# Stores to DRAM scratch issued from GpSimd's queue, and GpSimd's own work moved to ScalarE and VectorE

## The chip, the cores and the metric

The kernel runs on one core of one Trainium2 chip. The metric is the device time of one execution in microseconds (us). Three runs of the kernel before gave 2695.03 us in the median, from 2694.9 to 2701.88. The profile is one more execution of the same program.

The names of the engines in the profile: PE is TensorE's matmuls and PEld its weight loads, DVE is VectorE, ACT is ScalarE, POOL is GpSimd, SP is SyncE. SPq and POOLq are the queues of instructions of SP and POOL from which DMAs are issued. An engine works through its own instructions in order; before each it waits for the semaphores that the instruction names.

## The reference, cut to what matters

One layer of a streaming encoder for 2048 frames (SEQ) of width 1024, in float32:

```
h = rmsnorm(x, norm_mix_w)
u_b, u_c, u_h, z, xbc, dt_raw = split(h @ w_in)           # 5648 columns
y_a = u_b * conv3(u_c * u_h)                              # short gated convolution
xs, B, C = split(silu(conv4(xbc)))                        # causal, along the frames
dt = softplus(dt_raw + dt_bias)
y_b = ssd_scan(xs, dt, -exp(a_log), B, C) + d_skip * xs   # in chunks, a running state
y_b = grouped_rmsnorm(y_b * silu(z), norm_w)
x = x + concat(y_a, y_b) @ w_out                          # 2048 -> 1024
hid = square(relu(rmsnorm(x, norm_mlp_w) @ w_up))         # 1024 -> 4096
x = x + hid @ w_down                                      # 4096 -> 1024
return rmsnorm(x, final_norm_w)
```

## The kernel before

**Matrix products.** Operands are split in a high and a low part of the type fp32r, `hi` by a cast on ScalarE and `lo` by a subtraction on VectorE, and one float32 product is three matmuls: hi·hi, hi·lo, lo·hi (`mm3`, lines L113 to L115, or L270 to L272). The large products are cut in two by two blocks and calculated with seven products in place of eight (`Seven.chain`); the sums of blocks that this needs are made on VectorE, for weights in `combine`, for activations in `prepare` and `sums`. Weights come from DRAM through `load_w` (a DMA into one of three `wraw` buffers, L95) and `split_w` (L100 on ScalarE, L101 on VectorE).

**Stages.** In the profile, times from the start of the span: 0 to 485 us the norm and the first half of the input projection; 485 to 985 its second half, with chunks 0 to 15 of the scan beside it; 985 to 1310 the output projection, with chunks 16 to 31 of the scan beside it; 1310 to 1440 the rest of the output projection and the entry into the MLP (its normed input is made, its first weights are loaded); 1440 to 2050 the first product of the MLP; 2050 to 2694 the second one and the final norm.

**DRAM scratch.** SBUF doesn't hold the activations, so most results of a stage are stored to DRAM and loaded by the next stage: the sums of the normed input (`hm_d`, `hn_d`, L373/L374), sums of weights (`sums_d`, L234/L240), outputs of the projection (`sz_d`, `ys_d`, `xs_d`, L506 and L651 to L726), the small arrays of the scan (`rd_d`, `dt_d`, L636/L638), the scan's result (`yn_d`, L1274), the residual stream (`x1_d`, named x_d in the profile, L1428), the hidden activations (`hid_d`, L825/L826, and `b12_d`, L822) and the unnormed end result of the first half (`fin_d`, L955). All these DMAs, loads and stores alike, are issued by SP. A store waits at the head of SP's queue until the engine that makes its data is done, and what stands behind it waits too.

**The convolutions.** `Proj.pair` copies the last two or three columns of the half before (`halo`, `halo_s`) in front of a tile, and `conv` and `short` copy the last columns of the new tile back: 80 copies of 128x3 or 128x2 elements on GpSimd (L643, L654, L672, L675).

**The scan.** `Scan.back` takes one of 32 chunks: matmuls `yo`, `st`, `yd` on TensorE; four instructions on VectorE (L1252 to L1255); two on GpSimd (L1258 adds the skip term, L1259 multiplies with the gate); the square on ScalarE (L1262), two sums on VectorE, the sum over partitions as a matmul into `pss` (L1268), the root and reciprocal, and the last product (L1273), which is stored (L1274).

**The output projection.** `Output.unit` runs 64 times, 24 matmuls each. A unit issues the load of the residual tile of the unit after it (L1407, three `xt` buffers; units 32 to 63 load what units 0 to 31 have stored), adds the product to its own (L1427) and stores it (L1428). Units 48 to 63 issue beside it `prepare` for the MLP, and units 62 and 63 its first weights (`load_w`, L95).

**What sets the order.** The kernel is written with the Tile framework. The Python code only issues the work; a scheduler of the framework puts each engine's instructions in an order of its own, by when it thinks that their operands are there, and sets the semaphores. So a change of an instruction's engine can move other instructions as well. DMAs of SP use eight semaphores in turn (DMAHW0 to DMAHW7 in the order below); DMAs of GpSimd have eight of their own (DMASW0 to DMASW7).

## Time and profile before

| | us |
|---|---|
| median of three runs | 2695.03 |
| span of the profiled execution | 2694.2 |
| TensorE busy with matmuls in it | 2610.2 |
| VectorE busy | 1979.4 |
| ScalarE busy | 1381.7 |
| GpSimd busy | 141.5 |
| 16 DMA engines, mean share of the span | 58% |

The profiled execution is as long as the runs' median, within 0.9 us. Rows of the windows view give one stretch of the span: start and end, its length, then busy time and number of instructions of PE, PEld, DVE, ACT and POOL, the granted clock of TensorE (1.00 is full speed), the mean busy share of the DMA engines and GB/s. Rows of the waits view say which engine and line stood idle for what, how long in total, how often, and the longest. In rows of the timeline the number in brackets is the engine's idle time ahead of the instruction, and what ended it; a "xN" at the end of a name means N such instructions in a row, with their time together. An issue of a DMA on SPq takes the time that stands in its row; the data arrive later.

### The profile page before, as it was taken

How to read it: one execution, taken by the hardware profiler on the slowest of the kernel's cores; microseconds unless marked ns; L12 is line 12 of the kernel's file. 1: busy time of each engine (PE TensorE's matmuls, PEld its weight loads, DVE VectorE, ACT ScalarE, POOL GpSimd, SP SyncE). 2: the span in 40 equal slices, each digit the busy share in tenths (PEclk: the TensorE clock that was granted, in tenths of full speed). 3: DMA queues.
4: the chain of work that ended last, by engine and by line, in shares of the span. 5: the costliest groups of instructions: out<-in, count | busy, mean ns of one | idle time of the engine just before them, and what ended most of it. 6: DMA issues, size and time to landing. Idle time of an engine off the chain costs nothing.

```text
span 2694.2 us, 33500 instructions
## 1 busy us (share of the span) xinstructions
PE 2610.2 (97%) x12024; PEld 2125.7 (79%) x12024; DVE 1979.4 (73%) x2687; ACT 1381.7 (51%) x2042; POOL 141.5 (5%) x162
## 2 busy tenths in 40 slices
PE   7999999999999999998999999999999999999998
PEld 5778888678887878776877788788887888888777
DVE  7997677667768766666658856765657887888985
ACT  6633345666567566757326445654545333334433
POOL 0000000011111001111000000000000000000001
PEclk9999999999999999999999999999999999999999
DMA  3575335555555588867596844644348544665752
GB/s 143 189 287 193 141 141 186 183 167 167 171 165 168 161 265 264 250 204 215 191 328 235 312 168 149 228 167 167 143 162 277 160 148 153 205 213 172 238 199 75
DMA packets 288262, 522.27 MB, mean 194 GB/s; under 512 B 25696, under 2 KB 141408, under 8 KB 288096
## 3 DMA queue, kind: packets, MB, share of 16 engines
q1 hardware_dynamic: 288096, 520.14, 57.8%
q8 instruction: 94, 1.54, 0.2%
q14 instruction: 72, 0.59, 0.1%
HBM read 349.65 MB, written 170.39 MB: 193 GB/s over the span
## 4 chain that ended last, share of the span: by engine, by line
PE 57%; issue 25%; DMA 7%; DVE 5%; ACT 3%; POOL 1%; SPq 1%; POOLq 0%; DVEq 0%; ACTq 0%
PE px L270 8%; PE px L272 8%; PE px L271 8%; PE py L270 4%; PE py L271 4%; PE py L272 4%; PE pm L113 3%; PE pm L114 3%; PE pm L115 3%; PE pw L270 2%; PE pw L272 2%; PE pw L271 2%; DMA dec<-rd_d 1%; DVE wlo L101 1%; PE yd L1243 1%
## 5 line engine op out<-in xcount | busy, mean ns | idle before, releaser
L270 PE MATMUL px<-uh,whi 128*128 128x512 f32 x1672 | 660.2, 395 | 27.3 <-DVE xt L1427 7.9
L272 PE MATMUL px<-uh,wlo 128*128 128x512 f32 x1672 | 654.1, 392 | 9.0 <-DVE wlo L101 9.0
L271 PE MATMUL px<-ul,whi 128*128 128x512 f32 x1672 | 653.9, 391 | 0.0
L270 PEld LDWEIGHTS px<-uh,whi 128*128 128x128 f32 x1672 | 315.7, 189 | 106.8 <-issue 16.4
L101 DVE TENSOR_TENSOR wlo<-wraw,whi 128x1024 fp32r<-128x1024 f32 x230 | 233.6, 1016 | 198.5 <-ACT whi L100 195.0
L272 PEld LDWEIGHTS px<-uh,wlo 128*128 128x128 f32 x1672 | 315.5, 189 | 78.3 <-DVE wlo L101 11.9
L271 PEld LDWEIGHTS px<-ul,whi 128*128 128x128 f32 x1672 | 315.9, 189 | 63.9
L100 ACT CAST whi<-wraw 128x1024 fp32r<-128x1024 f32 x230 | 203.1, 884 | 303.4 <-PE px L271 194.6
L100 ACT CAST whi<-s 128x1024 fp32r<-128x1024 f32 x210 | 219.2, 1044 | 226.8 <-PE py L271 89.9
L270 PE MATMUL py<-uh,whi 128*128 128x512 f32 x836 | 327.2, 391 | 2.2 <-ACT whi L100 2.2
L272 PE MATMUL py<-uh,wlo 128*128 128x512 f32 x836 | 325.7, 390 | 0.6 <-DVE wlo L101 0.5
L271 PE MATMUL py<-ul,whi 128*128 128x512 f32 x836 | 325.9, 390 | 0.0
L101 DVE TENSOR_TENSOR wlo<-s,whi 128x1024 fp32r<-128x1024 f32 x210 | 255.9, 1219 | 39.5 <-ACT whi L100 38.8
L113 PE MATMUL pm<-uh,whi 128*128 128x512 f32 (+1 forms) x648 | 252.9, 391 | 2.1 <-ACT uh L204 2.1
L114 PE MATMUL pm<-ul,whi 128*128 128x512 f32 (+1 forms) x648 | 249.1, 384 | 0.0
L115 PE MATMUL pm<-uh,wlo 128*128 128x512 f32 (+1 forms) x648 | 248.8, 384 | 0.0
L315 ACT CAST uh<-rh 128x1024 fp32r<-128x1024 f32 (+1 forms) x128 | 120.3, 944 | 144.2 <-PE py L272 123.0
L270 PEld LDWEIGHTS py<-uh,whi 128*128 128x128 f32 x836 | 156.9, 188 | 36.4 <-ACT whi L100 3.8
L272 PEld LDWEIGHTS py<-uh,wlo 128*128 128x128 f32 x836 | 156.9, 188 | 34.8 <-DVE wlo L101 1.9
L271 PEld LDWEIGHTS py<-ul,whi 128*128 128x128 f32 x836 | 157.0, 188 | 32.5 <-issue 0.2
L270 PE MATMUL pw<-uh,whi 128*128 128x512 f32 x418 | 163.6, 391 | 0.0
L272 PE MATMUL pw<-uh,wlo 128*128 128x512 f32 x418 | 163.2, 390 | 0.0
(215 smaller groups left out, 3798.8 us busy)
## 6 DMA issues: line engine op xcount, KB each, us to landing
hid_d<-e SPq DMA_DIRECT2D x96, 512.0 KB, 3.3
rh<-hid_d SPq DMA_DIRECT2D x96, 512.0 KB, 4.2
wraw<-w_in SPq DMA_DIRECT2D x68, 512.0 KB, 3.8
wraw<-w_up SPq DMA_DIRECT2D x64, 512.0 KB, 5.0
wraw<-w_down SPq DMA_DIRECT2D x104, 256.0 KB, 3.6
dec<-rd_d SPq DMA_DIRECT2D x32, 512.0 KB, 5.4
wraw<-w_out SPq DMA_DIRECT2D x32, 512.0 KB, 5.2
x_d<-xt SPq DMA_DIRECT2D x64, 256.0 KB, 3.7
```

Of the source, the lines that this page charges most:

```text
L100: nc.scalar.copy(hi, raw)
L101: eng.tensor_tensor(out=lo, in0=raw, in1=hi.bitcast(F32), op=ALU.subtract)
L113: nc.tensor.matmul(out, whi, hi, start=(k == 0), stop=False)
L114: nc.tensor.matmul(out, whi, lo, start=False, stop=False)
L115: nc.tensor.matmul(out, wlo, hi, start=False, stop=(k == nk - 1))
L270: nc.tensor.matmul(p, hi, h[0], start=bool(first and k == 0), stop=False, **kw)
L271: nc.tensor.matmul(p, hi, h[1], start=False, stop=False, **kw)
L272: nc.tensor.matmul(p, lo, h[0], start=False, stop=(k == len(g) - 1), **kw)
L315: nc.scalar.copy(p[i][0], t)
L1243: nc.tensor.matmul(yd[(i % 2) * 64 : (i % 2) * 64 + 64, (i // 2) * L : (i // 2 + 1) * L], byhead(t["xdt"])[:, i, :], t["dec"][:, i, :], st ...
```

## The change

- 419 DMAs that store to DRAM are issued by GpSimd (`nc.gpsimd.dma_start`) and no longer by SP: every store but the last ones of the kernel (L1070, in `norm_out`).
- The 80 halo copies of the convolutions run on ScalarE in place of GpSimd.
- The scan's two instructions on GpSimd (L1258, L1259; 32 times each) run on VectorE.

What GpSimd keeps of its own instructions are the constants at the start and the products of `norm_out` (L1065). Arithmetic, tiles, buffers and all loads are the same. Cut to one place of each kind:

```
@@ -231,13 +231,13 @@
             if kept is not None:
-                nc.sync.dma_start(kept[:, 0], s12)
+                nc.gpsimd.dma_start(kept[:, 0], s12)
...
@@ -370,8 +370,8 @@
                 for i in range(3):
-                    nc.sync.dma_start(self.stored[h][k][:, 2 * i : 2 * i + 2], ts[i])
-                nc.sync.dma_start(self.stored[h][k][:, 6], t4)
+                    nc.gpsimd.dma_start(self.stored[h][k][:, 2 * i : 2 * i + 2], ts[i])
+                nc.gpsimd.dma_start(self.stored[h][k][:, 6], t4)
...
         def conv(self, h, q, buf):
 
-            nc.gpsimd.tensor_copy(self.halo[:, q, 0:3], buf[:, TH : TH + 3])
+            nc.scalar.copy(self.halo[:, q, 0:3], buf[:, TH : TH + 3])
...
             for i, e in enumerate((e0, e1, e2)):
-                nc.sync.dma_start(hid_d[h][q][:, 2 * i : 2 * i + 2], e)
-            nc.sync.dma_start(hid_d[h][q][:, 6], t4)
+                nc.gpsimd.dma_start(hid_d[h][q][:, 2 * i : 2 * i + 2], e)
+            nc.gpsimd.dma_start(hid_d[h][q][:, 6], t4)
...
             t3 = t1.rearrange("p (j l) -> p j l", j=4)
-            nc.gpsimd.tensor_tensor(out=t3, in0=t3, in1=t["xd"], op=ALU.add)
-            nc.gpsimd.tensor_tensor(out=y, in0=t3, in1=y, op=ALU.mult)
+            nc.vector.tensor_tensor(out=t3, in0=t3, in1=t["xd"], op=ALU.add)
+            nc.vector.tensor_tensor(out=y, in0=t3, in1=y, op=ALU.mult)
...
             nc.vector.tensor_tensor(out=t, in0=pm, in1=t, op=ALU.add)
-            nc.sync.dma_start(x1_d[b][:, d], t)
+            nc.gpsimd.dma_start(x1_d[b][:, d], t)
```

The same edit stands at L506, L636, L638, L651, L713 to L726 (stores of the projection), L822, L955, L1110 (the first half of the output) and L1274.

What the edit does to the order is seen at two places. In the rows, each name carries the number of its tile, the shape follows, and the brackets hold the semaphores that are waited for.

The first place is SP's queue at the entry into the MLP, where units 61 to 63 of the output projection end and the first weights of the MLP (`wraw_11851`, `wraw_11853`) are loaded. Before:

```order
L1428 DMA x1_d3_80<-xt_11689 128x512 [waits DMAHW1_49]
L1407 DMA xt_11777<-x1_d3_80 128x512 [waits DMAHW2_49]
L1428 DMA x1_d2_79<-xt_11740 128x512 [waits DMAHW3_49,DVE_49]
L95 DMA wraw_11851<-w_up 128x1024
L1407 DMA xt_11822<-x1_d2_79 128x512 [waits DMAHW4_49,DMAHW0_49]
L1428 DMA x1_d3_80<-xt_11777 128x512 [waits DMAHW5_49,DMAHW1_49,DVE_49]
L95 DMA wraw_11853<-w_up 128x1024 [waits DMAHW6_49]
```

In the changed kernel the rows around the same two loads on SP's queue are these:

```order
L1407 DMA xt_11437<-x1_d3_80 128x512 [waits DMAHW1_49,DMASW2_49,DVE_49]
L360 DMA nb_11429<-x1_d0_77 128x512 [waits DMAHW2_49,DMASW3_49,DVE_49]
L95 DMA wraw_11851<-w_up 128x1024 [waits DMAHW3_49,DVE_49]
L360 DMA nb_11432<-x1_d1_78 128x512 [waits DMAHW4_49,DMASW4_49]
L360 DMA nb_11431<-x1_d1_78 128x512 [waits DMAHW5_49,DMASW5_49]
L360 DMA nb_11430<-x1_d0_77 128x512 [waits DMAHW6_49,DMASW6_49]
L1407 DMA xt_11484<-x1_d2_79 128x512 [waits DMAHW7_49,DMASW7_49]
L1407 DMA xt_11521<-x1_d3_80 128x512 [waits DMAHW0_49,DMASW0_49,DVE_49]
L360 DMA nb_11499<-x1_d0_77 128x512 [waits DMAHW1_49,DMASW1_49,DVE_49]
L95 DMA wraw_11853<-w_up 128x1024 [waits DMAHW2_49,DVE_49]
```

The stores of `xt` are gone from this queue, and the two loads of weights stand among the loads for units whose `xt` carry numbers about 11437 to 11521, where before they stood among those of `xt_11777` and `xt_11822`: counted in loads alone, they moved ahead by 21 to 27.

The second place is VectorE's queue in one chunk of the scan during the output projection. `state1` and `stmp` are the scan's, `ul0` and `xt` belong to the output projection. Before:

```order
L1254 TENSOR_TENSOR state1_3802<-state1_3802,st_10418 128x512 [waits DVE_49,PE_49]
L1255 TENSOR_TENSOR stmp_10429<-stmp_10429,yd_10420 128x512 [waits PE_49]
L1373 TENSOR_TENSOR ul0_10613<-ry_10476,uh0_10612 128x512 [waits DMAHW3_49,Activation_49]
L1271 RECIPROCAL srstd_10436<-srstd_10436 128x128 [waits Activation_49]
L1373 TENSOR_TENSOR ul0_10618<-ry_10476,uh0_10617 128x512
L1273 TENSOR_TENSOR y_10145<-y_10145,srstd_10436 128x512 [waits DMAHW1_49,DVE_49]
L1263 TENSOR_TENSOR stmp_10530<-stmp_10530 128x256 [waits Activation_49]
```

After:

```order
L1254 TENSOR_TENSOR state1_3802<-state1_3802,st_10418 128x512 [waits DVE_49,PE_49]
L1255 TENSOR_TENSOR stmp_10429<-stmp_10429,yd_10420 128x512 [waits PE_49]
L1373 TENSOR_TENSOR ul0_10613<-ry_10476,uh0_10612 128x512 [waits DMAHW0_49,Activation_49]
L1271 RECIPROCAL srstd_10436<-srstd_10436 128x128 [waits Activation_49]
L1258 TENSOR_TENSOR stmp_10429<-stmp_10429,xd_10085 128x512 [waits DMAHW1_49,DVE_49]
L1273 TENSOR_TENSOR y_10145<-y_10145,srstd_10436 128x512 [waits DVE_49]
L1259 TENSOR_TENSOR y_10341<-stmp_10429,y_10341 128x512 [waits DMAHW3_49,DMASW2_49,DVE_49]
L1373 TENSOR_TENSOR ul0_10618<-ry_10476,uh0_10617 128x512
L1427 TENSOR_TENSOR xt_10381<-pm_10447,xt_10381 128x512 [waits DMAHW2_49,DMASW1_49,PE_49]
L1263 TENSOR_TENSOR stmp_10530<-stmp_10530 128x256 [waits Activation_49]
```

The two instructions L1258 and L1259 stand between the scan's other instructions, and the sum L1263, which needs the square of L1259's result, comes behind one addition of the output projection (L1427) that stood later before.

## What the time will be, predicted before the change was run

> **What bounds the kernel now.** I read the totals first, then busy time by stage, then what TensorE waited for, then what SP's queue waited for. The totals and the six stages:
>
> ```profile
> PE 2610.2 (97%) x12024; PEld 2125.7 (79%) x12024; DVE 1979.4 (73%) x2687; ACT 1381.7 (51%) x2042; POOL 141.5 (5%) x162
> core 0: 2694.2 us, clock 0.992
> 0.00:485.00 485.00, 457.58 (x1990) 371.81 (x1991) 380.06 (x520) 233.69 (x303) 25.72 (x49) 0.99 0.51 185
> 485.00:985.00 500.00, 495.53 (x2457) 397.82 (x2456) 361.46 (x496) 322.67 (x542) 59.45 (x72) 1.00 0.55 172
> 985.00:1310.00 325.00, 310.24 (x1623) 248.97 (x1622) 206.32 (x310) 203.53 (x403) 47.73 (x32) 0.99 0.78 233
> 1310.00:1440.00 130.00, 120.50 (x520) 98.64 (x519) 87.78 (x109) 43.12 (x55) 0.00 (x0) 0.96 0.79 275
> 1440.00:2050.00 610.00, 604.58 (x2649) 496.99 (x2649) 416.63 (x542) 329.91 (x446) 0.00 (x0) 1.00 0.54 194
> 2050.00:2694.00 644.00, 621.78 (x2793) 511.46 (x2791) 527.17 (x714) 248.82 (x296) 8.59 (x9) 0.99 0.56 181
> ```
>
> TensorE bounds the kernel: it is busy for 2610.2 of 2694.2 us. No matmul is added or taken away, so at most the 84.0 us between the two can be won, of which some 27 us lie in the first stage (485 less 457.58) and 22 us in the last (644 less 621.78). VectorE, at 73%, comes second. These are the waits of TensorE that could hang on SP's queue or on VectorE's; the second group is the part from 20 to 485 us alone, the third 1310 to 1440, the last 2050 to 2680:
>
> ```profile
> PE px L272 <- DVE wlo L101: 9.0, 6, 3.1
> PE px L270 <- DVE xt L1427: 7.9, 1, 7.9
> PE pss L1268 <- DVE facc L1441: 7.0, 1, 7.0
> ...
> PE px L272 <- DVE wlo L101: 5.1, 3, 3.1
> PE px L270 <- ACT whi L100: 2.6, 1, 2.6
> ...
> PE px L270 <- DVE e L838: 1.5, 1, 1.5
> ...
> PE px L270 <- DVE acc L969: 6.4, 9, 1.3
> PE px L272 <- DVE wlo L101: 2.6, 1, 2.6
> PE px L270 <- ACT whi L100: 2.1, 1, 2.1
> ```
>
> They are small and spread out, with two of 7 to 8 us. The larger is the entry into the MLP, where the first product needs a buffer that the last addition L1427 sets free. What SP and VectorE did there:
>
> ```profile
> 1398.35 0.40 SPq L1428 DMA_DIRECT2D x_d<-xt  x1
> 1398.79 0.45 SPq L95 DMA_DIRECT2D wraw<-w_up  x1
> 1400.65 0.32 SPq L1407 DMA_DIRECT2D xt<-x_d  x1
> 1403.24 0.32 SPq L1428 DMA_DIRECT2D x_d<-xt  x1
> 1403.61 0.43 SPq L95 DMA_DIRECT2D wraw<-w_up  x1
> ...
> 1408.48 0.69 DVE L231 TENSOR_TENSOR s<-wraw 128x512 f32<-128x512 f32 x1 [1.24 <-DMA wraw<-w_up]
> ...
> 1411.57 2.36 DVE L101 TENSOR_TENSOR wlo<-s,whi 128x1024 fp32r<-128x1024 f32 x2 [0.46 <-ACT whi L100]
> 1413.85 4.63 DVE L316 TENSOR_TENSOR ul<-rb,uh 128x1024 fp32r<-128x1024 f32 x4
> 1418.39 0.69 DVE L1427 TENSOR_TENSOR xt<-pm,xt 128x512 f32<-128x512 f32 x1
> ```
>
> Each load of `w_up` was issued right behind a store `x_d<-xt`, which had stood at the head of the queue until its addition was done. VectorE then idled 1.24 us for the second load (issued 1403.61, used 1408.48), and had to do the weight sums, `wlo` and four `ul` in one piece before the last addition at 1418.39. TensorE resumed at 1419.22 with the granted clock down:
>
> ```profile
> 1413.00:1423.00 10.00, 3.78 (x9) 3.04 (x10) 8.97 (x9) 5.88 (x7) 0.00 (x0) 0.52 0.84 282
> ```
>
> The four running microseconds of this row went at 0.52, which costs about 2 us on top of the 7.9 us.
>
> **The change part by part.** First the stores. Waits of SP's queue that are for data to be stored, and then what one store costs and how long it takes to land:
>
> ```profile
> SPq L825 <- DVE e L208: 258.4, 85, 11.1
> SPq L1428 <- DVE xt L1427: 51.7, 38, 3.2
> SPq L1407 <- DMA x_d<-xt: 51.6, 31, 3.8
> ...
> x_d<-xt SPq DMA_DIRECT2D x64, 256.0 KB, 3.7
> xt<-x_d SPq DMA_DIRECT2D x32, 256.0 KB, 4.3
> ```
>
> SP loses 419 issues of 0.32 to 0.40 us (the rows of L1428), some 134 to 168 us of queue time, and the waits above (258.4 and 51.7 us of them) go to GpSimd's queue, where no load stands behind them. SP's own time is worth nothing by itself, since nothing but DMAs runs there; it counts only where a load came late. In the first product of the MLP, TensorE is busy 604.58 of 610 us in spite of the 258.4 us, so there they are worth at most 5.4 us; I take nothing. The wait of 51.6 us is a dependence (a load of what a store has just written) and stays.
>
> What is late at the entry into the MLP is the weights. In the new order both loads of `w_up` stand 21 to 27 loads earlier on SP's queue, and VectorE's weight sums stand ahead of the last units' work. In the stage before, 1310 to 1440, VectorE has 130 − 87.78 = 42 us free and can take the sums and `wlo` there. What is left then at the border is the last addition (0.69 us) and the hops around it, about 1.4 us as in the smallest waits above (1.3, 1.5), so 6.5 us of the 7.9 go. The clock, which fell only in long idling, should then not fall: another 2 us. The wait of 1.5 us on L838 right behind it I leave.
>
> In the first stage, VectorE is busy 78% and the 5.1 and 2.6 us of waits for weights lie where `prepare` stores `hm_d` between the loads: loads that no longer queue behind those stores are worth perhaps a fifth of 7.7 us, 1.5 us. The same kind at the start of the last stage, 2.6 and 2.1 us, I put at 0.8 us, and another 0.6 us near 481, where the stage's last loads of `hm_d` come.
>
> What does a store cost on GpSimd? No row of before shows a DMA issued there. The nearest ones are SP's 0.32 us per issue, GpSimd's smallest copy and its large instructions:
>
> ```profile
> L643 POOL COPY halo<-buf 128x3 f32<-128x3 f32 x24 | 9.3, 390 | 271.2 <-DVE buf L692 271.2
> L1258 POOL TENSOR_TENSOR stmp<-stmp,xd 128x512 f32<-128x512 f32 x32 | 46.8, 1462 | 558.6 <-DVE stmp L1255 315.5 <-issue 115.8 <-DMA bc<-xs_d 35.4
> L1259 POOL TENSOR_TENSOR y<-stmp,y 128x512 f32<-128x512 f32 x32 | 44.9, 1403 | 2.5
> L1253 DVE TENSOR_TENSOR state<-state,dd 128x512 f32<-128x512 f32 x32 | 21.9, 684 | 0.2 <-PE yo L1238 0.2
> L1211 ACT COPY btok<-ptb 128x128 f32<-128x128 f32 x32 | 8.5, 267 | 0.0
> ```
>
> I take 0.5 us, a little above the copy, since an issue moves no data through the engine. Ends: 0.32 us and 1.46 us. 419 stores are then 134, 210 or 612 us of a queue that is otherwise nearly empty. A store is late by 0 to 1.1 us (1.46 less 0.32), or, since it no longer waits behind loads on SP, somewhat early. Who feels it is the loop over `x_d` in units 32 to 63 alone: addition 0.69, store 3.7, load 4.3, together 8.7 us. The load is issued one unit ahead, and what it loads was stored by a unit at least three before; a unit is 24 matmuls, at 610/2649 = 0.230 us each 5.5 us, so three are 16.6 us, with 7.9 us to spare. A delay of 1.1 us is hidden: nothing.
>
> By the Trainium skill, page "DMA: Bandwidth & Descriptors", section Specifications, the first byte of a transfer from GpSimd's software descriptors comes at about 1 us against about 0.6 us for the hardware's; no run here shows it yet, and by an estimate from it a store would land 0.4 us later, which leaves the sum as it is.
>
> Halo copies: 80 leave GpSimd (0.39 us each) for ScalarE, at 0.27 us by the copy L1211, together 21 us on an engine that is busy 51%. In the two stages where they lie it is busy 233.69 of 485 and 322.67 of 500. A copy could hold up the cast `whi` behind it by 0.27 us; if one in eight did so at a moment when TensorE waits, that is 10 × 0.27 = 2.7 us; I take 0.7 us, and 0 to 5 us as ends.
>
> The scan: 64 instructions leave GpSimd, where they took 1.46 and 1.40 us, for VectorE at 0.69 us: 64 × 0.684 = 43.8 us, half each in 485 to 985 and 985 to 1310. VectorE goes there from 361 to 383 of 500 us and from 206 to 228 of 325 us, still under 77%. What hides them is this free time; if it is gone where a burst stands, 1.37 us per chunk shows. On the other side the chunk's chain gets shorter by 1.46 + 1.40 − 1.37 = 1.5 us and one change of engine. The chain counts at the other large wait, `pss` behind `facc`:
>
> ```profile
> 1248.29 1.26 POOL L1258 TENSOR_TENSOR stmp<-stmp,xd 128x512 f32<-128x512 f32 x1 [13.85 <-DVE stmp L1255]
> 1246.98 0.55 SPq L1173 DMA_DIRECT2D dec<-rd_d x1
> 1253.38 0.40 ACT L1218 ACTIVATE dec<-dec,dd 128x128 f32<-128x128 f32 x1 [1.82 <-DMA dec<-rd_d]
> 1254.30 0.69 DVE L1441 TENSOR_TENSOR facc<-sq,facc 128x512 f32<-128x512 f32 x1 [1.68 <-ACT sq L1440]
> ```
>
> `dec` was issued late, at 1246.98, and all else waited behind it on ScalarE. With a shorter chain and an SP queue without stores it could come 2 us earlier, and the wait of 7.0 us shrink by that. Against it I set 1.3 us for VectorE's 1.37 us showing in about one chunk of 32. Of the stage I keep −2 for that wait and, with the copies' 0.7, +2 for costs.
>
> The sum: −6.5 − 2 (entry into the MLP) − 1.5 − 0.6 (first stage) − 0.8 (last stage) − 2 (scan) + 2 = −11.4 us. Against the profiled 2694.2 that is 2682.8; the runs' median is 0.8 us above the span, so 2683.6, said as 2683.5 us.
>
> **The rivals.**
>
> *No change.* TensorE's waits are bursts of VectorE, and loads that come earlier only wait in their buffers: with three `wraw` buffers a load can be issued early only when a buffer comes free, and the new order may find it taken. Then the 7.9 us stay but for 1.24 us of idling, and the rest is noise: −1.2 + 2 − 2 gives about 2694, with 2691 to 2699 around it. Against it speaks that the store at 1398.35 stands directly ahead of the load at 1398.79. By the Trainium skill, "DMA: Bandwidth & Descriptors", section "Issuing engines are not separate DMA queues", another issuing engine saves only the sequencer's time for the issue; that is this rival's mechanism, and the 258.4 us of SP that cost TensorE at most 5.4 us agree with it.
>
> *Slower: stores queue up on GpSimd.* Its queue is in order as SP's is. In units 48 to 63 the stores of `hn_d` (four per step of `prepare`) and of `x_d` share it. If a store takes 2 us there in place of 0.5, four of them hold an `x_d` store up for 8 us and lengthen its own issue by 1.7; with 7.9 us to spare, the loop is short by 1.8 us in each of 16 units: 29 us less the gain of 11.4, about 2713. It decides from about 1.65 us per store on (four are 6.6 us, the longer issue 1.3). For it speaks that GpSimd's instructions in the profile take about twice VectorE's time (1462 against 684 ns); against it that an issue moves no tile, and the copy of 390 ns.
>
> *Slower: VectorE too full.* If the 1.37 us per chunk shows in each of 16 chunks of the output projection, where the additions L1427 set free the buffers that TensorE needs, that is 22 us less the gain of 11.4: about 2705. VectorE's 63% in that stage speaks against it.
>
> **How the numbers follow.** My forecast has a chance of 0.52: about half the sum rests on one wait whose release moved plainly in the order. No change has 0.18. Stores that queue up have 0.20, since their price has no row at all, and a full VectorE 0.10. A difference of 0.3%, 8.1 us, is about what a measurement of this kernel can tell from no change, so 2686.9 and 2703.1 divide the cases: faster 0.52, same 0.18, slower 0.30. My forecast's own range is 2668 (the 7.0 us too and half of the first stage's waits gone, −26) to 2687 (the clock not won, copies at 4 us). The range reaches over no change to the full VectorE, with some spread, to 2708; outside are most of the stores that queue up and the forecast's own ends.
>
> **What would show it.** The entry into the MLP right: loads of `w_up` issued on SP well before 1395 us, and the wait of `px` on L1427 under 2 us with the clock near 1.0 in those 10 us. Stores right: issues on POOLq around 0.5 us, landing within 1 us of 3.7, no wait of L1407 longer than now. Copies right: about 0.27 us each on ScalarE, and waits for `whi` no longer. Scan right: L1258 and L1259 at 0.69 us on VectorE, and less than 2 us more of waits of TensorE for VectorE between 485 and 1310. The prediction is wrong if an issue on GpSimd takes over 1.5 us, if TensorE's busy time itself changes, or if VectorE's other instructions get longer while GpSimd issues stores.

## The result, and the profile after

The changed kernel takes 2741.41 us in the median (2737.48 to 2743.27, four runs), beside 2697.03 us for the kernel before on the same chip: a ratio of 1.016, with a 95% interval from 1.0145 to 1.0174. It is slower by 44 us, where the prediction said 11 us faster, and it lies above the range.

The totals of the changed kernel's page, with the row of its core, answer to the first rows of the prediction:

```profile
PE 2626.3 (96%) x12024; PEld 2136.6 (78%) x12024; DVE 2010.2 (73%) x2751; ACT 1390.4 (51%) x2122; POOL 242.8 (9%) x437
core 0: 2740.0 us, clock 0.984
```

TensorE does the same 12024 matmuls. Its busy time grew by 16.1 us, since a matmul takes longer at a lower granted clock, and its idle time by some 30 us. Both have the same places here: in the rows below the clock is 1.00 in 150 us without a wait, and 0.50 and 0.51 in two short pieces that lie right behind waits of 8.4 and 7.2 us; a matmul takes 150 / 664 = 0.23 us at 1.00 and 4.81 / 11 = 0.44 us at 0.50. The windows view of the kernel before, 150 us in the middle of the MLP's first product:

```profile
1570.00:1720.00 150.00, 150.00 (x662) 123.89 (x661) 90.60 (x119) 75.81 (x104) 0.00 (x0) 1.00 0.41 146
```

The same view of the changed kernel, in the middle of that product, at its beginning, and two short pieces of the beginning:

```profile
1600.00:1750.00 150.00, 150.00 (x664) 124.24 (x663) 90.78 (x119) 75.84 (x105) 15.63 (x30) 1.00 0.41 150
1430.00:1565.00 135.00, 114.65 (x466) 92.56 (x467) 97.84 (x131) 63.83 (x85) 19.88 (x37) 0.89 0.70 246
1434.00:1439.00 5.00, 4.81 (x11) 3.80 (x12) 4.05 (x5) 1.72 (x2) 0.54 (x1) 0.50 0.80 229
1547.00:1556.00 9.00, 5.30 (x12) 3.74 (x13) 9.00 (x15) 3.28 (x4) 1.62 (x3) 0.51 0.77 259
```

In these 150 us in the middle of the product nothing is lost: TensorE is busy for 150 of 150 us with the stores on GpSimd, as it was before. The loss stands at the beginning, where the clock is 0.89 in the mean and 0.50 and 0.51 in the two pieces. Where the 44 us arise is read from the start of one and the same instruction of VectorE in two traces. The table gives its time in the kernel before and how much later it starts (us) in the changed kernel and in four of the experiments told below. Each column is one trace: the kernel "stores alone, order held" and the one with stores from ScalarE (told below) do not differ before the MLP, yet at the last unit of the output projection they stand at +7.6 and +12.1, so a difference of less than 5 us between columns says little.

| place (instruction) | before | changed | moved compute alone | stores alone, order held | all of it, order held | all of it, SP's order free |
|---|---|---|---|---|---|---|
| first unit of the output projection (L1427) | 990 | +5.3 | −2.1 | +1.5 | 0.0 | +4.7 |
| last chunk of the scan (L1254) | 1292 | +6.5 | −9.5 | +5.5 | −5.7 | −0.4 |
| last unit of the output projection (L1427) | 1418 | +15.0 | −10.3 | +7.6 | −3.1 | +7.1 |
| MLP up, 25th addition (L838) | 1594 | +30.3 | −11.7 | +11.1 | −0.7 | +11.5 |
| the same, 46th | 1727 | +33.6 | −11.0 | +11.2 | −0.7 | +11.2 |
| the same, 67th | 1864 | +34.9 | −11.7 | +12.8 | +1.4 | +15.1 |
| the same, 91st | 2017 | +34.9 | −11.6 | +12.8 | +1.4 | +15.1 |
| MLP down, 7th addition (L969) | 2073 | +39.5 | −11.2 | +13.3 | +2.1 | +19.1 |
| the end (L1049) | 2648 | +45.3 | −12.0 | +22.0 | +10.4 | +26.2 |

In the changed kernel, 24 us of the 45 arise between the end of the scan and the first quarter of the MLP's first product, where the normed input is made, stored and loaded again (`prepare`). The rest comes in four pieces of some 5 us each: in the input projection, later in the MLP's first product, at the border to its second, and in the last third of that product.

The largest waits of TensorE in the changed kernel, after the one at the start:

```profile
PE px L270 <- DVE e L838: 12.8, 5, 3.6
PE px L270 <- DVE acc L969: 11.3, 8, 3.6
PE px L272 <- DVE wlo L101: 10.3, 3, 7.2
PE px L270 <- DVE xt L1427: 8.4, 1, 8.4
PE pss L1268 <- DVE facc L1441: 7.8, 1, 7.8
PE px L270 <- ACT s L689: 7.3, 5, 3.5
PE pm L113 <- DVE xt L1427: 6.8, 4, 3.1
PE px L270 <- DVE buf L692: 4.2, 1, 4.2
```

The waits view of its VectorE and of SP's queue, those that changed most:

```profile
DVE nb L364 <- DMA nb<-x_d: 29.8, 10, 5.7
...
SPq L95 <- DVE wlo L101: 813.3, 118, 16.1
SPq L1407 <- DMA x_d<-xt: 156.2, 46, 8.3
```

TensorE waits for nothing that is new in kind: mostly evictions and additions of VectorE that set its buffers free (L838, L969, L692, L1427). VectorE's own wait for loads ahead of the normed input's first step grew from 5.7 us in the kernel before to 29.8. SP's wait for free weight buffers grew from 296.4 to 813.3 us and its wait at the reload of the residual stream from 51.6 to 156.2. These two are no measure of the loss: SP no longer stands at stores and so stands at the next load, and with the old order held (below) they are still 734.6 and 119.1 us.

How the one leads to the other is seen at the first such place. The rows are the timeline's around 155 us in the changed kernel, VectorE's and the matmul that waited:

```profile
154.79 0.75 DVE L364 SCALAR_TENSOR_TENSOR nb<-nb,cv,facc 128x512 f32<-128x512 f32 x1 [5.35 <-DMA nb<-x]
155.46 0.68 DVE L692 TENSOR_TENSOR buf<-px,s 128x512 f32<-128x512 f32 x1
...
156.19 0.65 PE L270 MATMUL px<-uh,whi 128*128 128x512 f32 x1 [4.24 <-DVE buf L692]
```

VectorE's queue held L364, which needs a load, ahead of the addition L692, which sets a buffer of TensorE free. VectorE stood 5.35 us for the load (of the input x, which no store feeds), and TensorE stood 4.24 us for the addition. In the timeline of the kernel before, the additions L692 of this product stand ahead of L364:

```profile
150.36 0.69 DVE L692 TENSOR_TENSOR buf<-px,s 128x512 f32<-128x512 f32 x1 [1.96 <-PE px L272]
153.15 0.69 DVE L692 TENSOR_TENSOR buf<-py,s 128x512 f32<-128x512 f32 x1 [2.10 <-PE py L272]
153.75 1.41 DVE L364 SCALAR_TENSOR_TENSOR nb<-nb,cv,facc 128x512 f32<-128x512 f32 x2
```

### The profile page after: what moved, and what is told of

Its sections match the earlier page's. It is cut to its first block, busy times and chain, and to the rows that moved or that the text cites. A ratio compares the mean times of both kernels' runs of the same rounds, so it can differ in the third digit from the quotient of the medians.

```text
span 2740.0 us, 33639 instructions
## 1 busy us (share of the span) xinstructions
PE 2626.3 (96%) x12024; PEld 2136.6 (78%) x12024; DVE 2010.2 (73%) x2751; ACT 1390.4 (51%) x2122; POOL 242.8 (9%) x437
## 4 chain that ended last, share of the span: by engine, by line
PE 41%; issue 40%; DMA 8%; DVE 6%; POOL 2%; ACT 2%; SPq 0%; POOLq 0%; DVEq 0%; ACTq 0%
PE px L270 6%; PE px L271 6%; PE px L272 6%; PE py L270 3%; PE py L272 3%; PE py L271 3%; PE pm L113 3%; PE pm L114 2%; PE pm L115 2%; PE pw L272 1%; PE pw L271 1%; PE pw L270 1%; DVE wlo L101 1%; DVE ul L316 1%; DMA rb<-hn_d 1%
## 5 line engine op out<-in xcount | busy, mean ns | idle before, releaser
L270 PE MATMUL px<-uh,whi 128*128 128x512 f32 x1672 | 666.5, 399 | 51.9 <-DVE e L838 12.8
L272 PE MATMUL px<-uh,wlo 128*128 128x512 f32 x1672 | 659.1, 395 | 10.3 <-DVE wlo L101 10.3
L272 PEld LDWEIGHTS px<-uh,wlo 128*128 128x128 f32 x1672 | 318.9, 191 | 80.1 <-DVE wlo L101 12.1
```

The costliest lines, as they stand in the source:

```text
L270: nc.tensor.matmul(p, hi, h[0], start=bool(first and k == 0), stop=False, **kw)
L272: nc.tensor.matmul(p, lo, h[0], start=False, stop=(k == len(g) - 1), **kw)
```

## The experiments

My theory after the result was that the stores carry the whole loss, in two shares: they land later, and the scheduler, which took them to cost less, made a worse order of it. The rivals were a VectorE that is too full, and a GpSimd queue that is too slow by itself. "Order held" means that a function at the end of the build draws an edge from each instruction of an engine to the next, in the order of another build; the edges set the order of issue and are of the kind that has no semaphore:

```
+def pin(nc, tc):
...
+    at = {i.name: i for i in nc.cur_bb.bb.instructions}
+    for engine, names in json.loads(zlib.decompress(base64.b85decode(ORDER))).items():
+        here = [at[f"I-{n}"] for n in names if f"I-{n}" in at and engine in str(at[f"I-{n}"].engine)]
+        for a, b in zip(here, here[1:]):
+            tc.add_manual_dep(b, a.name, info, reason="order")
```

In the traces of the kernels held like this, the loads on SP and the instructions of the other three engines do stand in the order that they were held to, without exception. The kernel before with only these edges was not run, so that the edges cost nothing by themselves is not shown. The traces speak for it: in the held kernel told last, whose stores of the hidden activations are on SP, the MLP's first product loses nothing from its 25th addition to its end (+6.6 us behind the kernel before at both ends, within 0.3 us).

### Stores alone, compute alone

The first kernel takes only the stores of the change (against the changed kernel):

```
-            nc.scalar.copy(self.halo[:, q, 0:3], buf[:, TH : TH + 3])
+            nc.gpsimd.tensor_copy(self.halo[:, q, 0:3], buf[:, TH : TH + 3])
...
-            nc.vector.tensor_tensor(out=t3, in0=t3, in1=t["xd"], op=ALU.add)
-            nc.vector.tensor_tensor(out=y, in0=t3, in1=y, op=ALU.mult)
+            nc.gpsimd.tensor_tensor(out=t3, in0=t3, in1=t["xd"], op=ALU.add)
+            nc.gpsimd.tensor_tensor(out=y, in0=t3, in1=y, op=ALU.mult)
```

> Only the 419 stores go to GpSimd's queue; the halo copies and the scan's two instructions stay on GpSimd. Theory 'stores' (the whole loss comes from the stores, of 1310 to 1555 us above all): 2735 to 2745 us, as the changed kernel. Theory 'VectorE too full': 2690 to 2702 us, since the compute that moved is back.

Measured: 2748.22 us beside 2698.15 for the kernel before, ratio 1.0183 (1.0153 to 1.0214). This is 3 us above the range of the first theory and far from the second.

The second takes only the other half, the same lines the other way round, with all stores on SP.

> Only the halo copies and the scan's two instructions are moved; all stores stay on SP. Theory 'stores': 2690 to 2700 us, no difference from before. Theory 'VectorE too full': 2725 to 2740 us.

Measured: 2686.29 us, ratio 0.9958 (0.9941 to 0.9975). It is faster than the kernel before, and 4 us below both ranges. The stores carry the loss, and a VectorE too full is out: the moved compute wins 12 us. A third kernel moves the scan's two instructions alone:

```
-            nc.gpsimd.tensor_tensor(out=t3, in0=t3, in1=t["xd"], op=ALU.add)
-            nc.gpsimd.tensor_tensor(out=y, in0=t3, in1=y, op=ALU.mult)
+            nc.vector.tensor_tensor(out=t3, in0=t3, in1=t["xd"], op=ALU.add)
+            nc.vector.tensor_tensor(out=y, in0=t3, in1=y, op=ALU.mult)
```

> Only the scan's two instructions go to VectorE; halo copies stay on GpSimd and all stores on SP. Theory 'the scan's shorter chain wins the 12 us': 2684 to 2690 us. Theory 'the halo copies' part is half of it': 2690 to 2695 us.

Measured: 2690.02 us beside 2698.62, ratio 0.9965 (0.995 to 0.998). Most of the gain is the scan's; whether the halo copies add the rest can't be told, since the two intervals overlap.

Where the gain is from stands in VectorE's waits. In the kernel before:

```profile
DVE stmp L1263 <- ACT stmp L1262: 65.6, 25, 5.8
```

With the compute moved, this wait, and the groups of the moved instructions:

```profile
DVE stmp L1263 <- ACT stmp L1262: 17.9, 12, 3.7
...
L1258 DVE TENSOR_TENSOR stmp<-stmp,xd 128x512 f32<-128x512 f32 x32 | 21.8, 683 | 0.4
L1259 DVE TENSOR_TENSOR y<-stmp,y 128x512 f32<-128x512 f32 x32 | 22.0, 686 | 0.7
L643 ACT COPY halo<-buf 128x3 f32<-128x3 f32 x24 | 4.6, 191 | 36.7 <-DVE buf L692 36.6
```

VectorE took 43.8 us of work and lost 47.7 us of waiting. While GpSimd did the chunk's two steps, VectorE stood at L1263, whose square comes from their result, and everything behind L1263 stood with it. VectorE's waiting is time of TensorE only in part: TensorE's own waits in the output projection with its chunks of the scan (985 to 1310 us, and 10 us earlier in the faster kernel) fell from 14.8 to 9.0 us, and in the table that stretch wins 7.4 of the 12 us. That the shorter wait at L1263 is what shortened them is argued, not shown.

### Which stores: the two that are reloaded at the costly place

The changed kernel with the stores of the residual stream and of the normed input back on SP:

```
-                    nc.gpsimd.dma_start(self.stored[h][k][:, 2 * i : 2 * i + 2], ts[i])
-                nc.gpsimd.dma_start(self.stored[h][k][:, 6], t4)
+                    nc.sync.dma_start(self.stored[h][k][:, 2 * i : 2 * i + 2], ts[i])
+                nc.sync.dma_start(self.stored[h][k][:, 6], t4)
...
-            nc.gpsimd.dma_start(x1_d[b][:, d], t)
+            nc.sync.dma_start(x1_d[b][:, d], t)
```

> The changed kernel, but the stores of the residual stream (L1428) and of the normed input (L373, L374) are back on SP; the other 299 stores are on GpSimd. Both theories of the stores: 2690 to 2705 us, since the only loops from store to load in 1310 to 1555 us run over these. If the hidden activations' stores (5.1 us to landing) hold the additions L838 up: 2712 to 2725 us.

Measured: 2739.38 us, ratio 1.0148 (1.0118 to 1.0178). Both expectations missed: nothing came back. (307 stores stay on GpSimd here, 112 are back; the expectation says 299.) With the order left to the scheduler, every such variant is a new order, so what the two loops cost by themselves can't be read from it, and from here on the order was held.

### Order held

Only the stores on GpSimd, and the loads on SP and all instructions of VectorE, ScalarE and TensorE in the order of the kernel before (the stores-alone kernel with `pin` called at its end):

> Only the stores are on GpSimd, and the loads on SP and the instructions of VectorE, ScalarE and TensorE are held in the very order of the kernel before. Theory 'order' (the scheduler's new order, with weight loads ahead of the loads of the normed input, makes those late): 2685 to 2700 us. Theory 'landing' (stores from GpSimd land later, 4.4 us against 3.7 for the residual and 5.1 against 3.3 for the hidden activations, and what loads them or reuses their buffers waits): 2728 to 2745 us.

Measured: 2723.81 us, ratio 1.0083 (1.0058 to 1.0109). Between the two theories: about half of the loss stays with the old order (25.7 us against 2698.15), so it goes with the stores themselves, and the other half (2748.22 less 2723.81, 24 us) is the order.

The full change, in the order of the compute-alone kernel:

> The changed kernel in full, with loads on SP and the instructions of VectorE, ScalarE and TensorE held in the order of the kernel that moved the compute alone (2686 us). Theory 'landing plus order' (two shares that add up, as 2724 against 2698 us for the landing alone and 2748 against 2724 us for the order): 2705 to 2716 us, that is 2686 plus about 25. Theory 'the shares do not add' (moved compute only helps where the stores stand on SP): 2722 to 2735 us.

Measured: 2708.15 us beside 2698.62, ratio 1.0034 (1.0019 to 1.005). The shares add up: 2686 and some 22, where the other pair gave 25.7. Now the full change with only the instructions of VectorE, ScalarE and TensorE held, and SP's order free (`pin` without the entry for SP):

> The changed kernel in full, with only the instructions of VectorE, ScalarE and TensorE held in the order of the kernel that moved the compute alone; SP's loads stay in an order of the scheduler's own (262 of 1043 places differ from that kernel's). With SP held as well it was 2708 us, with nothing held 2741. Theory 'VectorE's order' (instructions that need a late load stand ahead of those that free TensorE's buffers): 2705 to 2716 us. Theory 'SP's order' (weight loads that wait for a buffer stand ahead of the loads of the normed input): 2730 to 2742 us.

Measured: 2721.37 us beside 2698.25, ratio 1.0088 (1.0059 to 1.0117). It is between the two: of the 33 us from 2708 to 2741, SP's order of loads makes about 13 and the other engines' order about 20. The division is rough: it goes by which order was set free first, and SP's order in this kernel is not quite the changed kernel's (in the traces, by line and tile name, 182 of its 1019 loads stand in another place than in the kernel held in full, and 66 in another than in the changed kernel).

### What makes a store from GpSimd cost anything

With the order held there is no other change than the issuing queue, and the place of a store among GpSimd's own instructions, which the kernel of 2724 us still has in that queue. In the full change these have moved away, and the stores cost 22 us in place of 26, so they are a small part of it at most. First I suspected where a late landing comes from, and issued the hidden activations' stores from ScalarE:

```
-                nc.gpsimd.dma_start(hid_d[h][q][:, 2 * i : 2 * i + 2], e)
-            nc.gpsimd.dma_start(hid_d[h][q][:, 6], t4)
+                nc.scalar.dma_start(hid_d[h][q][:, 2 * i : 2 * i + 2], e)
+            nc.scalar.dma_start(hid_d[h][q][:, 6], t4)
```

> As the kernel with stores on GpSimd in the order of before (2724 us), but the 131 stores of the hidden activations (L822, L825, L826) are issued by ScalarE. What it tells is where the late landing is from. Theory 'software descriptors': L825's stores land in 3.2 to 3.8 us, as from SP (3.3), and the time is 2712 to 2722 us. Theory 'a second queue': loads and stores share the 16 DMA engines in turn once they stand in two queues, so they land in 4.6 to 5.4 us, as from GpSimd (5.1), and the time is 2720 to 2732 us.

Measured: 2758.04 us, ratio 1.0221 (1.0194 to 1.0249). The last number in a row of the list of DMAs is the median time from issue to landing. In the kernel before:

```profile
hid_d<-e SPq DMA_DIRECT2D x96, 512.0 KB, 3.3
```

With the stores on GpSimd and the order held:

```profile
hid_d<-e POOLq DMA_DIRECT2D x96, 512.0 KB, 5.1
```

With these stores on ScalarE, and behind it what TensorE waited for from 1580 to 1760 us in this kernel:

```profile
hid_d<-e ACTq DMA_DIRECT2D x96, 512.0 KB, 5.3
...
PE px L270 <- ACT s L835: 5.9, 8, 1.2
```

The late landing is not GpSimd's alone: from ScalarE it is as late. The time rose by 34 us more and lies outside both ranges; in the middle of the product TensorE now waits for ScalarE's copies L835, which stand in one queue with the stores. From 1420 to 2080 us this wait is 22.4 us in all, where the order-held kernel with all stores on GpSimd has 0.3.

The timeline shows what the stores meet. In the order-held kernel with all stores on GpSimd, SP issues a weight load 0.23 us after the first store of a group:

```profile
1615.04 0.53 POOL L825 DMA_DIRECT2D hid_d<-e  x1 [15.88 <-DVE e L208]
...
1615.27 0.33 SPq L95 DMA_DIRECT2D wraw<-w_up  x1
```

In the kernel before, the load stood behind the stores on SP:

```profile
1603.28 2.29 SPq L825 DMA_DIRECT2D hid_d<-e  x3
1606.00 0.32 SPq L826 DMA_DIRECT2D hid_d<-t  x1
1606.37 1.12 SPq L95 DMA_DIRECT2D wraw<-w_up  x1
```

To take this collision away and leave the stores on GpSimd, SP was made to wait as before: in each store's old place it reads a few numbers of the stored tile.

```
+    def store(dst, src):
+        nc.gpsimd.dma_start(dst, src)
...
+        head = src[0:1, :, 0:8] if len(src.shape) == 3 else src[0:1, 0:8]
...
+        PROBES.append(nc.sync.dma_start(seen, head).ins.name)
```

> As the kernel with the stores on GpSimd and the order of before (2724 us), but at each place where a store stood in SP's queue SP now issues a read of 8 or 16 numbers from the tile that is stored, into a scratch of its own: SP waits for the same data at the same places as before, and the loads behind start no earlier than before, while the 419 stores themselves go out from GpSimd. Theory 'collision' (loads that SP no longer holds back start together with the stores and share the 16 DMA engines, so that the stores land late): the hidden activations' stores land in 2.6 to 3.8 us and the time is 2692 to 2708 us. Theory 'GpSimd's queue' (a store issued from there lands late by itself): they land in 4.6 us or more and the time is 2718 to 2730 us.

Measured: 2723.26 us beside 2699.08, ratio 1.0094 (1.0068 to 1.0121). The two signs disagree. The landing of `hid_d<-e` fell to 3.7 us, as the collision theory had it, and the time did not move. So the collision makes up most of these 96 stores' lateness (5.1 to 3.7, of 3.3). What it is worth to end it stays open: the 32 smaller stores `hid_d<-t` landed later still (6.2 us, against 5.5 with the order held and 3.5 from SP), the 419 reads are transfers themselves whose cost no run shows, and there was little to win, since the order-held kernel lost only 2 us from the 25th addition to the second product (+11.1 to +13.3 in the table). What is left with SP's waits restored is a later start of GpSimd's stores and perhaps a later landing. The start is plain between the end of an addition and the issue of its store. In the kernel before:

```profile
1406.56 0.68 DVE L1427 TENSOR_TENSOR xt<-pm,xt 128x512 f32<-128x512 f32 x1
1407.27 0.32 SPq L1428 DMA_DIRECT2D x_d<-xt  x1
```

In the changed kernel:

```profile
1419.35 0.68 DVE L1427 TENSOR_TENSOR xt<-pm,xt 128x512 f32<-128x512 f32 x1
1420.44 0.54 POOL L1428 DMA_DIRECT2D x_d<-xt  x1 [7.71 <-DVE xt L1427]
```

SP issued 0.03 us after the end (1406.56 + 0.68 = 1407.24), GpSimd 0.41 us after it (1420.03). In the medians over all stores of this line it is 0.03 and 0.41 us too, and the landing behind it 3.7 against 4.3 us in the last experiment: there a store from GpSimd is done about 0.4 + 0.6 = 1.0 us later. The start is the same, within 0.01 us, in the traces of all kernels told here. The landing is less sure: from SP the stores of this line landed in 3.3 to 4.6 us, by kernel, and from GpSimd in 3.8 to 4.8.

Two last kernels, both in the order of before, divide the stores: on SP, or alone on GpSimd, are the 168 whose data or buffers are wanted again in the same stage (L1428, L373, L374, L1274, L955, L1110).

> Stores on GpSimd in the order of before, but the 168 that are loaded again or whose buffers are reused within the same stage are on SP: residual (L1428), normed input (L373, L374), the scan's result (L1274), end results of the first half (L955, L1110). 251 stores stay on GpSimd: hidden activations, outputs of the projection, weight sums, small arrays. Theory 'loops' (a store from GpSimd starts 0.4 us later and lands 0.3 to 1 us later, and only loops from store to load inside a stage feel it): 2695 to 2705 us. Theory 'all stores': 2708 to 2718 us, about 251/419 of the 25 us.

Measured: 2709.3 us beside 2699.55, ratio 1.0037 (1.0024 to 1.0051), with 251 stores on GpSimd.

> The reverse, in the order of before: only the 168 stores of the loops (L1428, L373, L374, L1274, L955, L1110) are on GpSimd. Theory 'loops': 2715 to 2726 us, nearly the whole 25 us. Theory 'all stores': 2704 to 2713 us.

Measured: 2715.27 us, ratio 1.0064 (1.0047 to 1.0082), with 168. The losses, 9.8 and 15.7 us, add up to that of all 419. The 168 make 62% of it, 0.09 us per store against 0.04 for the rest. So neither theory holds: the loops seem to weigh more, though the two intervals touch, and the others count as well.

No stage carries the share of the stores alone. In the table's two columns with the order held, each counted from the kernel whose order it has, about half of it (11 us) has arisen by the 25th addition of the MLP's first product, some 2 us more by the end of that product, and 8 to 9 us in the second, where GpSimd issues only the 24 stores L955 and L1110. But the kernel with the scan alone moved, whose stores are all on SP, loses 6 us in that stretch as well, so this last part can't be laid to the stores with certainty.

### A faster kernel

The compute-alone kernel beats both. One more step was tried on it, the MLP's first weights two units earlier:

```
-            if n == 62:
+            if n == 60:
                 ahead = mlp.weights(mlp.load_cols(w_up, (0, 1)))
                 next(ahead)
-                ws = take(ahead, 2)
-            elif n == 63:
+            elif n == 61:
+                ws = take(ahead, 2)
+            elif n == 62:
                 ws += take(ahead, 1)
```

> The kernel that moved the compute alone (2686 us), with the MLP's first weights loaded two units earlier and split one unit earlier, so that VectorE does the last addition L1427 of the output projection two `ul` and no weight work later than it could. If the wait of TensorE at the entry into the MLP (7.1 us) is VectorE's weight work: it falls to 2 to 4 us, and the time is 2680 to 2684 us. If it is the loads of the normed input: 2685 to 2688 us.

Measured: 2687.49 us beside 2698.62, ratio 0.9964 (0.9946 to 0.9981): no gain over 2686. The wait at the entry fell only from 7.1 to 6.0 us, so VectorE's weight work is a small part of it, and in the two traces the first product had lost the difference again by its 25th addition (−13.3 against −10.3 us at the last unit, −11.1 against −11.7 there). At the entry VectorE then waited for ScalarE's `uh`, which waited 2.7 us for a load of the normed input (`rb`).

## Why the prediction was wrong, point by point

**The sum.** Against the kernel before, in medians (those of the kernel before beside each experiment lie between 2697.0 and 2699.6, so each figure is good to 2 or 3 us): moved compute −12, stores from GpSimd in an unchanged order +22 (order-held full change less compute alone; +26 by the other pair), SP's new order +13, the other engines' new order +20. Together +43, measured +44; they are differences along one row of kernels, so that they add up is no test of them. My sum had −2 + 2 for the compute, 0 for the delay of the stores, and −11 for all that the new order and the freed queue of SP would bring. The lower end of my range, −26, does not follow from the two terms named beside it: with 7.0 in place of 2 and half of 7.7 in place of 1.5, the −11.4 becomes about −19.

**The step that failed first: "a delay of 1.1 us is hidden: nothing".** The price itself was right: I took 0.5 us for an issue and 0 to 1.1 us of delay. An issue took 0.54 us in the median, and the residual landed in 4.4 us in place of 3.7. But I asked only whether the loop over `x_d` closes in time, and gave it 7.9 us to spare. I did not name what stands behind the waiting load on SP. With the order held, where nothing but the queue differs, this term was not 0 but 22 to 26 us. At the entry into the MLP these rows of the changed kernel, which has the new order too, show how a late store reaches TensorE; the store is the one at 1420.44 above:

```profile
1426.28 0.32 SPq L1407 DMA_DIRECT2D xt<-x_d  x1
1426.69 2.48 SPq L308 DMA_DIRECT2D rb<-hn_d  x4
...
1431.14 1.04 ACT L315 CAST uh<-rb 128x1024 fp32r<-128x1024 f32 x1 [4.19 <-DMA rb<-hn_d]
...
1432.22 1.23 DVE L316 TENSOR_TENSOR ul<-rb,uh 128x1024 fp32r<-128x1024 f32 x1 [3.39 <-ACT uh L315]
1433.36 0.68 DVE L1427 TENSOR_TENSOR xt<-pm,xt 128x512 f32<-128x512 f32 x1
...
1434.19 0.76 PE L270 MATMUL px<-uh,whi 128*128 128x512 f32 x1 [8.37 <-DVE xt L1427]
```

The reload L1407 was issued when the store had landed, 5.8 us after the store's issue. Four loads of the normed input stood behind it, `uh` and `ul` waited for these, and the addition that frees TensorE's buffer stood behind `ul`. The delay of one store doesn't have to break its own loop; it has only to reach a queue's head.

Here it broke the loop as well. What the reload waits for is not its data, as I wrote of the 51.6 us, but one of the three `xt` buffers: in the traces it is never issued before the store of the unit three before has landed, and within 0.1 us behind it in 17 of the 32 reloads before and in 29 of 32 in the changed kernel. So the loop runs over three units, as I took it, but not with 16.6 us: from the end of the addition at 1419.35 to the end of TensorE's last matmul of the unit three later (1425.8) it had 5.8 us, and the start of the store, its landing and the reload took 9.4 (0.4, 5.8 and 3.1), so the tile came some 3.6 us late. My 7.9 us to spare was worked out from the mean length of a unit, and VectorE's additions come in bursts (two of them, L1427, start at 1419.35 and 1420.55).

**"−6.5 − 2 (entry into the MLP)".** The mechanism came as forecast as far as the weights: the first three loads of `w_up` were issued at 1355.49, 1369.45 and 1385.68 us, 22 to 43 us earlier than before, and VectorE's weight sums went ahead. The wait still was 8.4 us and the clock fell to 0.50. My step "what is left then at the border is the last addition" failed: what was late next was the normed input. The run with earlier weights says the same for the kernel without the stores' trouble, 6.0 of 7.1 us left. With the order held and the stores on GpSimd this wait was longer in both pairs of traces: 9.3 us against 7.9 in the kernel before, and 10.1 against 7.1 with the compute moved.

**The order.** I read the new order for one gain and counted no cost of it: 33 us. That the order is their cause is shown by the held kernels. How they come about is shown at 156 us, where an instruction that needs a late load stands ahead of an addition that frees a buffer, and argued for the rest. Why the scheduler made this order is not shown; that it took the stores to cost less and drew what depends on them forward is a guess, and the load at 156 us depends on no store.

**First stage, "−1.5 − 0.6".** It became about +5 by 990 us, with the wait at 156 us and one of 3.5 us near 487. Whether the order or the stores made it can't be told: with the order of before held, the traces of the five kernels stand at +1.5 to +5.6 us there.

**The scan, "−2" and "+2" for costs.** The sign was right and the size wrong. L1258 and L1259 took 0.683 and 0.687 us on VectorE as said, and the halo copies 0.18 to 0.19 us on ScalarE where I said 0.27. The gain was about 12 us and not 0: I counted the shorter chain for one wait and set 1.37 us per chunk of VectorE's time against it, and left out that VectorE itself had been waiting 65.6 us at L1263 for that chain.

**The rivals.** Stores that queue up on GpSimd for 2 us each did not happen: an issue took 0.54 us. A full VectorE is out. Of the signs that I had named, two came: the wait at L1407 grew from 51.6 to 156.2 us, and TensorE's busy time changed, by the clock. "No change" had its mechanism partly right: in the middle of the MLP the freed queue won nothing, which agrees with the Trainium skill, "DMA: Bandwidth & Descriptors", section "Issuing engines are not separate DMA queues", that another issuing engine saves the time of the issue alone (TensorE 150 of 150 us in both kernels). The right rival, that the order gets worse, was not among mine.

## What to carry to other kernels

Moving a store to an idle queue is not free: price the start and landing of the store, then ask what waits behind each instruction that needs it, on every in-order queue up to the engine that bounds the kernel. Where a scheduler makes the order, test the change once with the old order held; here that split one number into −12, +22 and +33, and only the −12, the moved compute, was worth keeping. Work moved onto a busy engine cost nothing here, where that engine had been waiting for just this work.

## What was not expected of the hardware

- In the rows of the profile, a DMA issued from GpSimd began 0.41 us after the end of its producer, one from SP 0.03 us after it (medians over the 64 stores of L1428); the issue itself took 0.54 us against 0.33.
- 512 KB stores of the hidden activations landed in 3.3 us from SP, in 5.1 from GpSimd and in 5.3 from ScalarE, and in 3.7 from GpSimd once SP held its loads back. For these stores most of the lateness is thus the traffic beside them.
- The halo copies of L643, 128x3 elements, took 0.39 us on GpSimd and 0.19 us on ScalarE; those of the other three lines took 0.49 to 0.67 us on GpSimd and 0.18 to 0.19 us on ScalarE.
